# Down projection: operand pairs of the first group made inside the direct column jobs; final rows: a group's squares issued after the next group's roundings

## The chip, the core and the metric

The kernel runs on one core of a Trainium2 chip. A core has five engines with their own in-order instruction streams: TensorE (PE in the profile, with its weight loads as PEld), VectorE (DVE), ScalarE (ACT), GpSimd (POOL) and SyncE (SP). Here SP only issues transfers, and POOL issues those that add into their destination. The metric is the device time of one execution in microseconds; the time before is the median of three runs.

## The reference, cut to what matters

One encoder layer on 512 tokens of width 2048, all in float32. The first part (normalisation, input projection, two kinds of sequence mixing, output projection, residual) is not touched. The change lies in the last part:

```python
h = rmsnorm(x, ffn_norm_w[l])
x = x + (jax.nn.silu(h @ w_gate[l]) * (h @ w_up[l])) @ w_down[l]
return rmsnorm(x, final_norm_w)
```

`w_gate` and `w_up` are 2048 x 5632, `w_down` is 5632 x 2048. With g for the product in the brackets, the down projection is g (512 x 5632) times `w_down`. The result is added to x, and every row is then normalised over its 2048 values.

## The kernel before, in words

**Precision.** A float32 operand is rounded to a high part on ACT (a copy to the fp32r type), and DVE subtracts that from the operand to give the low part. A product is then three matmuls: high by high, high by low, low by high. So each operand that reaches PE has first cost one ACT instruction and one DVE instruction. The text calls this pair of instructions a rounding.

**How w_down is tiled.** The 5632 rows of `w_down` are 44 tiles of 128 rows, taken as 22 pairs of tiles, numbered 0 to 21. The 2048 output columns are four column blocks c of 512. g lies in device memory, one pair to an entry (`gd`).

- *Pairs 0 and 1: the direct column jobs.* Four jobs, one for each c (`run_job`, L273; its matmuls are L303 to L305). A job has four steps i, one for each tile, and each step is 12 matmuls over 512 columns. Ahead of step i come `before_down` (L1463) and then `st.split`, which rounds the half piece of `w_down` that is used two or three steps later (L201 on ACT, L202 on DVE). At the job's end `evac_down` (L1457) copies four PSUM banks out with ACT, and POOL adds them into `xd`.
- *Pairs 2 to 19: the class `Down`.* It uses a seven-product scheme in place of eight on 2 x 2 blocks. For each pair q, seven operands are formed from g (B11, B21, B22, T1 to T4), and for each pair and column block the weights get sums of their own. One step i of `run` (pair q, column block c) is 7 x 2 x 3 = 42 matmuls over 256 columns (L1625 to L1627). The steps follow in ten runs r: X = pairs 2 to 7 for c = 0, 1, 2; X and Y = pairs 8 to 14 for c = 3; Y for c = 2 and 1; Y and Z = pairs 15 to 19 for c = 0; Z for c = 1, 2 and 3. The operands of X thus serve runs 0 to 3.
- *Pairs 20 and 21: the final rows* (`finish`), described below.

**What a step of Down needs.** The weights of step i are loaded (L1141, SP), summed (`sums`: L1157 to L1159, DVE) and rounded (`split`: L1169 on ACT, L1174 on DVE) up to three steps ahead, in the shared slots `s4` (20 of 128 x 1024). Four of these slots hold the weights of a step until its matmuls have read them, and the roundings for a later step go into slots set free in that way. The operands of a pair come out of the generator `operands` (from L1534), one piece of work for each call of `make`:

- the first call only loads two pairs of g (L1542, SP);
- step 1 of a pair: four 128 x 256 additions or subtractions on DVE (L1556 to L1559);
- step 2: two roundings (L1568 and L1569, and a first L1571 and L1572), and the load of a further pair;
- step 3: two more roundings (L1571, L1572). The next call enters the pair in `self.x` and goes on to step 1 of the next pair.

Before a pair is begun, the generator asks that its number is not above `self.upto` and that at least `self.gap` (13) of the 62 slots `s2` (128 x 512) are free. Otherwise the call does nothing. A pair keeps seven `s2` slots until its last run. `make(1)` is called once in the last unit of the gate and up products (`down_start`, L1434) and once in each of the 16 steps of the direct jobs (`before_down`). `run` calls it, behind the roundings of the weights, until the pair of its step is there, and then up to two times more.

`self.upto` is 0 when `Down` is built, and the first pair has the number 2. `run` sets it before each step: to 14, the last pair of Y, up to run 5, and to 19 from run 6 on.

**The final rows.** `finish` takes the 512 tokens as four rows t of 128. A group is one row and one column block: 12 matmuls over 512 columns (`products`, L1797 to L1799), then `residual` (L1449, DVE, reads the bank and adds into x1), then `squares` (L409, ACT, the sum of squares of the result). Rows 0 and 1 go together through the four column blocks, then row 2, then row 3. The last eight half pieces of `w_down` are rounded (L201, L202) in the first four groups, two to a group. `later` (L1780 to L1785) ends a row: the reciprocal root from the four sums of squares (ACT and DVE, one element to a partition), four multiplications on DVE (L1784) and the stores on SP. `run_urgent` puts left-over work of the last run of `Down` between the groups (L1689, DVE).

Engines take their instructions in the order in which the program issues them, and slots are handed out and put back in that order too; an instruction that writes a slot waits until the last readers of it are done.

Of the kernel before, what the change touches and what calls it, by code (L numbers as in the profile page):

```python
# [114 lines left out]
def put(*slots):  # L115
    for s in slots:
        if s.home is not None:
            s.home.free.append(s.i)


def layer(nc, tc, x, attn_norm_w, w_in, rel_table, gw_f, gb_f, gw_b, gb_b, gla_norm_w, w_out,
# [7 lines left out]
    with tc.manual_schedule(), \  # L129
# [30 lines left out]
        class Stream:  # L160


            def __init__(self):
                self.pieces = []
                self.halves = []
                self.n_dma = self.n_conv = 0
                self.limit = 3
                self.held = 0
                self.until = None
                self.big = None  # L170
# [38 lines left out]
        st = Stream()  # L209
# [25 lines left out]
        def run_urgent():  # L235
            while urgent:
                try:
                    next(urgent[0])
                    break
                except StopIteration:  # L240
                    urgent.popleft()
# [165 lines left out]
        def squares(c, t, tiles, ss):  # L407
            junk = s2.get()
            act.activation(junk.t, tiles[t].t, AF.Square, accum_out=ss[:, t * 4 + c:t * 4 + c + 1])  # L409
            put(junk)  # L410
# [3 lines left out]
        ss2, sum2, rstd2 = small[:, 32:48], small[:, 48:52], small[:, 52:56]  # L414
# [593 lines left out]
        x1 = {}  # L1008
# [472 lines left out]
        class Down(Blocks):  # L1481
# [3 lines left out]
            def __init__(self, X, Y, Z):  # L1485
                self.runs = [(0, X), (1, X), (2, X), (3, X + Y), (2, Y), (1, Y), (0, Y + Z), (1, Z), (2, Z), (3, Z)]
                self.pairs = X + Y + Z
                self.drop = {q: r for r, part in ((3, X), (6, Y), (9, Z)) for q in part}
                self.begin([(r, q) for r, (c, part) in enumerate(self.runs) for q in part], 1, 256)
                self.x, self.parts, self.m, self.pre, self.seen = {}, {}, {}, [], set()  # L1490
                self.most, self.upto, self.gap = 4, 0, 13
                self.making = self.operands()

            def source(self, r, q):
# [200 lines left out]
            def run(self):  # L1695
                for i, (r, q) in enumerate(self.seq):
                    c, part = self.runs[r]
                    n = part.index(q)
                    left = len(part) - 1 - n if self.summed(r) else None
                    self.load()  # L1700
                    self.sums(i)
                    self.split(i)
                    if left != 0:
                        self.sums(i + 1)
                        if r > 6 and n == 0:
                            self.split(i + 1)
                        self.sums(i + 2)
                        self.split(i + 1)
                        self.part(i + 3)
                        if left == 1:  # L1710
                            self.split(i + 2)
                            self.sums(i + 3)
                        elif r != 3 and not self.by_dma(i + 2) and len(s4.free) > 4:
                            self.sums(i + 3)
                            self.split(i + 2)
                    self.upto = self.pairs[-1] if r > 5 else self.runs[4][1][-1]
                    while q not in self.x:
                        self.make(1)
                    self.gap = 10 if r == 6 else 13
                    self.make(2 if r == 3 else (r == 6) + i % 2)  # L1720
                    if n == max(len(part) - 5, 0) and r + 1 < len(self.runs) and self.summed(r + 1):
                        self.fetch(r + 1)
                    if self.summed(r) and n == (1 if r == len(self.runs) - 1 else len(part) - 2):
                        x1[c] = [s2.get() for _ in range(4)]
                        for t in range(4):
                            pool.dma_start(out=x1[c][t].t, in_=xd[4 * c + t])
                    self.products(i)
                    if left == 0:
                        self.part(i + 3)
                    else:  # L1730
                        run_urgent()
                    if r == len(self.runs) - 1:
                        if n == 0:
                            g_load(LAST // 2)
                            g_load(LAST // 2 + 1)
                        if n == 1:
                            st.until, st.limit, st.big = None, 1, tail_first
                            st.load()
                            g_split(LAST // 2)
                        if n == 2:  # L1740
                            g_split(LAST // 2 + 1)
                            st.limit = 4
                            st.split(tail_first + 2)
                        if n == 3:
                            st.split(tail_first + 8)
# [24 lines left out]
        def finish():  # L1770
# [5 lines left out]
            upto = [first + 8]  # L1776
# [11 lines left out]
            def products(t, c, b, cols):  # L1788
                tok = slice(t * P, (t + 1) * P)
                o = b.t[:, cols]  # L1790
                for k in range(per):
                    if t < 2 and k % 2:
                        upto[0] += 1
                        st.split(upto[0])
                    _, _, wh, wl = st.halves[first + c * per + k]
                    xh, xl = gT[LAST + k]
                    mm(o, xh.t[:, tok], wh.t[:, cols], start=k == 0, stop=False, skip_group_check=True)  # L1797
                    mm(o, xh.t[:, tok], wl.t[:, cols], start=False, stop=False, skip_group_check=True)
                    mm(o, xl.t[:, tok], wh.t[:, cols], start=False, stop=k == per - 1, skip_group_check=True)  # L1799
# [8 lines left out]

            def run():
                whole = slice(0, 512)  # L1810
                for rows in ((0, 1), (2,)):
                    for c in range(4):
                        for t in rows:
                            b = ps.get()
                            products(t, c, b, whole)
                            run_urgent()
                            residual(c, t, b)
                            squares(c, t, x1[c], ss2)
                    for t in rows:
                        ys = [s2.get() for _ in range(4)]  # L1820
                        later(t, ys)
                        put(*ys, *(x1[c][t] for c in range(4)))
                t = 3
                ys = []
                sm, m, r, q = sum2[:, t:t + 1], scr[0][:, 0:1], rstdf[:, t:t + 1], scr[1][:, 0:1]
                for c in range(4):
                    ys.append(s2.get())
                    for n in range(2 if c == 3 else 1):
                        cols = slice(256 * n, 256 * n + 256) if c == 3 else whole
                        b = ps.get()  # L1830
                        products(t, c, b, cols)
                        if c == 3 and n == 1:
                            dve.tensor_reduce(sm, ss2[:, 11:15], op=OP.add, axis=mybir.AxisListType.X)
                            dve.tensor_scalar(sm, sm, 1.0 / D, EPS, op0=OP.mult, op1=OP.add)
                        at_ = 11 + c + n
                        part(t, c, b, cols, ss2[:, at_:at_ + 1], ys[c])
                dve.tensor_scalar(m, ss2[:, 15:16], 1.0 / D, sm, op0=OP.mult, op1=OP.add)
                act.activation(q, m, AF.Ln)
                act.activation(r, q, AF.Exp, scale=-0.5)
                dve.scalar_tensor_tensor(q, r, m, r, op0=OP.mult, op1=OP.mult)  # L1840
                dve.tensor_scalar(q, q, -0.5, 1.5, op0=OP.mult, op1=OP.add)
                dve.tensor_tensor(m, r, q, op=OP.mult)
                for c in (1, 0, 2, 3):
                    o = ys[c]
                    if c == 1:
                        act.activation(o.t, o.t, AF.Copy, scale=m)
                    else:
                        dve.tensor_scalar(o.t, o.t, m, None, op0=OP.mult)
                    (act if c in (1, 3) else sp).dma_start(
                        out=out[t * P:(t + 1) * P, c * 512:(c + 1) * 512], in_=o.t)  # L1850
                put(*ys, *(x1[c][t] for c in range(4)))
# [48 lines left out]
```

## Time and profile before

| | |
|---|---|
| time, median of 3 runs | 2218.49 us (2217.82 to 2223.97) |
| profiled execution: its time | 2222.8 us |
| profiled execution: span of the trace | 2221.0 us |
| mean granted TensorE clock | 0.993 of full speed |
| busy: PE | 2184.1 us (98%) |
| busy: PEld | 1921.2 us (87%) |
| busy: DVE | 1587.3 us (71%) |
| busy: ACT | 1228.8 us (55%) |
| busy: POOL | 329.1 us (15%) |

All times are microseconds from the start of the span. The view by stretches gives the busy time of each engine within a stretch, with the number of instructions in brackets, then the granted TensorE clock (PEclk), the busy share of the DMA engines and the rate moved. The view by time has a row for an instruction, or for several of a kind, with its start, its length and, in square brackets, the idle time of its engine before it and what ended this. The view by groups gives the number of instructions of a line, their busy time, the mean length of one in ns, and the idle time before them. Instructions that follow each other overlap a little on PE, DVE and ACT, so the distance between two starts is shorter than the length that is given.

In this execution the direct column jobs run from 1723.6 to 1766.97, `Down` from there to 2165.28, and the final rows from 2165.28 to the end.

### The profile page before, as it was taken

The page shows a single profiled execution, that of the slowest core. Times are in us where ns is not written, and L with a number is a line of the kernel's source. Part 1 is how long each engine was busy: PE and PEld are TensorE (multiplying, and loading weights), DVE is VectorE, ACT ScalarE, POOL GpSimd, SP SyncE. Part 2 cuts the span into 40 slices and gives each one's busy share as a digit, 9 for nine tenths or more (in the row PEclk, how much of TensorE's full clock was granted, in tenths as well). Part 3 has the DMA queues.
Part 4 walks back from the last instruction along what each step waited for, and adds up shares of the span by engine and source line. Part 5 has one row for each costly group of instructions (what it writes and reads, how often), then busy time and mean ns, then how long its engine had stood idle before and what let it go on. Part 6 is the DMA issues. An engine that isn't in the chain of part 4 may idle for free.

```text
span 2221.0 us, 33659 instructions
## 1 busy us (share of the span) xinstructions
PE 2184.1 (98%) x12594; PEld 1921.2 (87%) x12594; DVE 1587.3 (71%) x2757; ACT 1228.8 (55%) x2040; POOL 329.1 (15%) x363
## 2 busy tenths in 40 slices
PE   9999999999999999999999999999999879999998
PEld 7888888888888888888888888888888679999996
DVE  4366665755566447888888888888888576878987
ACT  5344454444556346666666666666665544745653
POOL 0000000000000111222222222222222201211110
PEclk9999999999999999999999999999999979999999
DMA  6525634323234425898898888889888835958882
GB/s 207 159 84 148 166 91 132 93 86 95 86 95 158 155 83 138 192 209 202 198 207 197 203 204 206 200 200 208 200 205 221 189 133 153 271 163 220 239 288 102
DMA packets 256467, 376.78 MB, mean 170 GB/s; under 512 B 18063, under 2 KB 179519, under 8 KB 256304
## 3 DMA queue, kind: packets, MB, share of 16 engines
q1 hardware_dynamic: 188768, 252.03, 36.2%
q0 software_dynamic: 66352, 121.55, 28.1%
q8 instruction: 99, 1.62, 0.3%
q10 hardware_dynamic: 1184, 1.06, 0.1%
q14 instruction: 64, 0.52, 0.1%
HBM read 246.58 MB, written 35.19 MB: 127 GB/s over the span
## 4 chain that ended last, share of the span: by engine, by line
PE 91%; DVE 3%; issue 2%; DMA 1%; ACT 1%; POOL 1%; SPq 0%; DVEq 0%; ACTq 0%; POOLq 0%
PE pd L1302 22%; PE pd L1308 11%; PE ps L303 5%; PE ps L304 5%; PE ps L305 5%; PE ps L295 5%; PE ps L296 5%; PE ps L297 5%; PE pu L1627 5%; PE pu L1626 5%; PE pu L1625 5%; PE pe L1302 4%; PE pe L1308 2%; PE ps L529 1%; PE ps L537 1%
## 5 line engine op out<-in xcount | busy, mean ns | idle before, releaser
L1302 PE MATMUL pd<-a,b 128*128 128x512 f32 x2112 | 528.4, 392 | 0.8 <-DVE a L1063 0.8
L1302 PEld LDWEIGHTS pd<-a,b 128*128 128x128 f32 x2112 | 378.9, 188 | 67.0 <-DVE a L1063 1.2
L1308 PEld LDWEIGHTS pd<-a,b 128*128 128x128 f32 x2112 | 288.5, 190 | 21.6
L1625 PE MATMUL pu<-b,a 128*128 128x256 f32 x1008 | 290.2, 288 | 14.2 <-ACT a L1568 11.1
L1627 PE MATMUL pu<-b,a 128*128 128x256 f32 x1008 | 290.2, 288 | 7.9 <-DVE a L1569 6.0
L1308 PE MATMUL pd<-a,b 128*128 128x256 f32 x2112 | 294.9, 282 | 0.0
L202 DVE TENSOR_TENSOR a<-b,a 128x512 fp32r<-128x512 f32 x273 | 183.3, 686 | 151.6 <-ACT a L201 139.3
L1626 PE MATMUL pu<-b,a 128*128 128x256 f32 x1008 | 289.6, 287 | 0.4 <-DVE b L1174 0.4
L1209 POOL DMA_DIRECT2D b<-b x176 | 209.8, 1248 | 520.8 <-ACT b L1208 390.8
L1247 ACT CAST b<-b 128x1024 fp32r<-128x1024 f32 x176 | 185.3, 1053 | 166.2 <-DVE b L1233 138.5
L1248 DVE TENSOR_TENSOR b<-b,b 128x1024 fp32r<-128x1024 f32 x176 | 214.9, 1221 | 50.2 <-ACT b L1247 26.4
L1625 PEld LDWEIGHTS pu<-b,a 128*128 128x128 f32 x1008 | 197.9, 196 | 15.6 <-ACT a L1568 12.2
L1627 PEld LDWEIGHTS pu<-b,a 128*128 128x128 f32 x1008 | 197.9, 196 | 9.5 <-DVE a L1569 7.0
L1626 PEld LDWEIGHTS pu<-b,a 128*128 128x128 f32 x1008 | 197.9, 196 | 0.6 <-DVE b L1174 0.6
L201 ACT CAST a<-b 128x512 fp32r<-128x512 f32 x273 | 161.5, 618 | 46.4 <-PE ps L305 22.3
L1330 DVE TENSOR_TENSOR a<-pd,a 128x512 f32<-128x512 f32 x132 | 91.4, 692 | 95.7 <-ACT a L1329 95.7
L1208 ACT ACTIVATE b<-b 128x768 fp32r<-128x768 f32 x176 | 149.3, 848 | 4.7 <-PE ps L305 2.9
L1210 ACT CAST b<-b 128x768 fp32r<-128x768 f32 x176 | 145.4, 826 | 0.6 <-PE ps L305 0.6
L1329 ACT COPY a<-pd 128x512 f32<-128x512 f32 x132 | 77.6, 588 | 101.9 <-PE pd L1308 101.9
L1169 ACT CAST b<-b 128x768 fp32r<-128x768 f32 x88 | 78.8, 940 | 99.6 <-issue 77.3
L1174 DVE TENSOR_TENSOR b<-b,b 128x768 fp32r<-128x768 f32 x88 | 94.3, 1090 | 46.2 <-ACT b L1169 42.5
L1230 DVE TENSOR_TENSOR b<-b 128x512 f32<-128x512 f32 x176 | 120.4, 684 | 0.0
(284 smaller groups left out, 4419.0 us busy)
## 6 DMA issues: line engine op xcount, KB each, us to landing
b<-b POOLq DMA_DIRECT2D x204, 384.0 KB, 5.8
b<-in_w_gate_dram SPq DMA_DIRECT2D x88, 512.0 KB, 4.2
b<-in_w_up_dram SPq DMA_DIRECT2D x88, 512.0 KB, 4.5
b<-in_w_down_dram SPq DMA_DIRECT2D x88, 512.0 KB, 5.8
b<-in_w_in_dram SPq DMA_DIRECT2D x48, 512.0 KB, 4.6
b<-in_w_in_dram SPq DMA_DIRECT2D x94, 256.0 KB, 4.2
b<-in_w_out_dram SPq DMA_DIRECT2D x32, 512.0 KB, 5.6
a<-a SPq DMA_DIRECT2D x96, 128.0 KB, 2.4
```

The costliest lines, as they stand in the source:

```text
L201: act.copy(h[2].t, r)
L202: dve.tensor_tensor(h[3].t, r, h[2].f, op=OP.subtract)
L1208: act.activation(lo.t, r, AF.Copy, scale=-1.0)
L1209: pool.dma_start(out=lo.f, in_=r, accum_op=OP.add)
L1210: act.copy(hi.t, r)
L1247: act.copy(hi.t, self.S[i].t)
L1248: dve.tensor_tensor(lo.t, self.S[i].t, hi.f, op=OP.subtract)
L1302: mm(o, wh.t[:, p, k], x_.t.rearrange("p s t -> p (s t)"), start=first and p == 0, stop=False, skip_group_check=True)
L1308: mm(o[:, 256:512], wl.t[:, p, k], x_.t[:, 0], start=False, stop=last and p == 1, skip_group_check=True)
L1625: mm(o, xh[:, t], wh, start=first and not loaded and h == 0, stop=False, skip_group_check=True)
L1626: mm(o, xh[:, t], wl, start=False, stop=False, skip_group_check=True)
L1627: mm(o, xl[:, t], wh, start=False, stop=last, skip_group_check=True)
```

## The change: what it does

`Down` is built with `self.upto` at 14, the last pair of Y. `run` sets `self.upto` from run 6 on alone. So a call of `make` in the direct jobs no longer does nothing, where 13 slots are free.

In the final rows, both roundings of a group are issued ahead of its 12 matmuls, where they stood ahead of the second and the fourth tile; they are the same instructions, and on ACT and DVE they keep their order among themselves. The squares of a group are put on a list and issued after the residual of the next group, that is, behind the roundings of the next group. The last squares of a set of rows are issued before `later`.

```diff
@@ class Down, __init__
-                self.most, self.upto, self.gap = 4, 0, 13
+                self.most, self.upto, self.gap = 4, Y[-1], 13
@@ class Down, run
-                    self.upto = self.pairs[-1] if r > 5 else self.runs[4][1][-1]
+                    if r > 5:
+                        self.upto = self.pairs[-1]
                     while q not in self.x:
                         self.make(1)
@@ finish, products
+                if t < 2:
+                    upto[0] += 2
+                    st.split(upto[0])
                 for k in range(per):
-                    if t < 2 and k % 2:
-                        upto[0] += 1
-                        st.split(upto[0])
                     _, _, wh, wl = st.halves[first + c * per + k]
@@ finish, run
                 whole = slice(0, 512)
+                todo = deque()
                 for rows in ((0, 1), (2,)):
                     for c in range(4):
                         for t in rows:
                             b = ps.get()
                             products(t, c, b, whole)
                             run_urgent()
                             residual(c, t, b)
-                            squares(c, t, x1[c], ss2)
+                            if todo:
+                                squares(*todo.popleft())
+                            todo.append((c, t, x1[c], ss2))
+                    squares(*todo.popleft())
                     for t in rows:
```

## The prediction

> **What bounds the kernel now.** I read the page first, then the busy time by stretches, then the groups within the one stretch where PE is not full, and last the rows by time around its gaps.
>
> ```profile
> span 2221.0 us, 33659 instructions
> ```
>
> ```profile
> core 0: us, PE busy (x) PEld busy (x) DVE busy (x) ACT busy (x) POOL busy (x), PEclk, DMA share, GB/s
> 1723.60:1734.48 10.88, 10.88 (x50) 9.00 (x49) 8.11 (x14) 5.48 (x10) 1.59 (x3) 1.00 0.92 356
> 1734.48:1745.36 10.88, 10.88 (x50) 9.01 (x49) 2.50 (x4) 4.80 (x9) 3.54 (x5) 1.00 0.68 98
> 1745.36:1756.24 10.88, 10.88 (x50) 9.01 (x49) 2.50 (x4) 4.80 (x9) 3.52 (x5) 1.00 0.66 96
> 1756.24:1766.97 10.73, 10.73 (x49) 8.68 (x47) 7.74 (x13) 5.40 (x9) 3.37 (x5) 1.00 0.82 147
> 1766.97:1832.00 65.03, 42.96 (x254) 40.18 (x254) 49.37 (x89) 28.77 (x48) 5.21 (x9) 0.79 0.49 142
> 1832.00:1862.15 30.15, 30.15 (x254) 30.15 (x253) 23.43 (x32) 15.21 (x22) 3.45 (x8) 1.00 0.43 135
> 2165.28:2189.60 24.32, 22.79 (x99) 17.79 (x98) 19.29 (x30) 12.86 (x28) 0.00 (x0) 1.00 0.17 63
> 2189.60:2211.66 22.06, 22.06 (x109) 18.58 (x107) 18.58 (x42) 6.71 (x22) 0.00 (x0) 1.00 0.40 143
> ```
>
> The first four rows are the four direct column jobs. PE is busy throughout, while in the second and third DVE works 2.50 us of 10.88. The fifth row is run 0 of `Down`: six steps, 252 matmuls, in 65.03 us at a mean clock of 0.79. The sixth row is the next six steps: the same 254 records in 30.15 us at full clock (0.1196 us a matmul, 5.02 us a step). So run 0 takes 65.03 - 30.15 = 34.9 us more than the same work does right behind it. The seventh row is the first eight groups of the final rows: 24.32 us, with PE idle for 1.5.
>
> Groups within 1766.97 to 1832:
>
> ```profile
> L1625 PE MATMUL pu<-b,a 128*128 128x256 f32 x85 | 29.0, 342 | 14.2 <-ACT a L1568 11.1 <-ACT a L1571 3.0
> L1627 PE MATMUL pu<-b,a 128*128 128x256 f32 x84 | 28.7, 342 | 7.9 <-DVE a L1569 6.0 <-DVE a L1572 1.8
> ...
> L1174 DVE TENSOR_TENSOR b<-b,b 128x768 fp32r<-128x768 f32 (+1 forms) x14 | 15.1, 1091 | 14.8 <-ACT b L1169 14.8
> ...
> L1572 DVE TENSOR_TENSOR a<-a,a 128x512 fp32r<-128x512 f32 x12 | 7.7, 686 | 0.0
> L1571 ACT CAST a<-a 128x512 fp32r<-128x512 f32 x12 | 6.9, 614 | 3.3 <-DVE a L1557 3.1 <-DVE a L1559 0.2
> ...
> L1556 DVE TENSOR_TENSOR a<-b 128x256 f32<-128x256 f32 x7 | 2.9, 420 | 0.0
> L1558 DVE TENSOR_TENSOR a<-b,a 128x256 f32<-128x256 f32 x7 | 2.9, 420 | 0.0
> L1569 DVE SCALAR_TENSOR_TENSOR a<-b,a 128x256 fp32r<-128x256 f32 x7 | 2.9, 419 | 0.0
> L1557 DVE TENSOR_TENSOR a<-b 128x256 f32<-128x256 f32 x7 | 2.9, 419 | 0.0
> L1568 ACT ACTIVATE a<-b 128x256 fp32r<-128x256 f32 x7 | 2.9, 412 | 0.0
> ```
>
> All of PE's idle time, 14.2 + 7.9 = 22.1 us, ends with a rounding of a pair's operands (L1568, L1569, L1571, L1572), none with weights. The other 34.9 - 22.1 = 12.8 us are matmuls at a lowered clock after these gaps.
>
> Why a pair is late at each step shows on ACT:
>
> ```profile
> 1784.07 1.78 ACT L1169 CAST b<-b 128x768 fp32r<-128x768 f32 x2 [7.52 <-PE pu L1627]
> 1785.75 0.41 ACT L1568 ACTIVATE a<-b 128x256 fp32r<-128x256 f32 x1
> 1786.07 0.60 ACT L1571 CAST a<-b 128x512 fp32r<-128x512 f32 x1
> ```
>
> ```profile
> 1786.22 0.39 PE L1625 MATMUL pu<-b,a 128*128 128x256 f32 x1 [2.23 <-ACT a L1568]
> ```
>
> L1169 rounds the weights of a step three ahead into slots that the finished step sets free, so ACT stands still until PE is through. The roundings of the pair that PE wants next are queued behind it. PE and ACT take turns, step after step.
>
> **The pairs, part by part.** The first call of `make` only loads. The 16 calls in the direct jobs then do three steps to a pair: pairs 2 to 6 are finished by the sixteenth call, which also does step 1 of pair 7. Slots: following the handing out and putting back in the code, the direct jobs leave 45 of the 62 `s2` slots free at the first call, 49 through the middle, and 51, 53 and 57 at the last three. With seven held for each finished pair, pair 6 begins with 49 - 28 = 21 free and pair 7 with 57 - 35 = 22; 13 are asked for, so every call does its step. Pair 7 gets its second and third steps in steps 1 and 3 of run 0 and is used in step 5. At the end of step 5 both kernels stand at the same place (pair 8 after its second step, 10 slots free); from there on the program is the same.
>
> *Cost of what moves.* By the rows above, a pair takes on DVE 4 x 0.42 + 0.42 + 3 x 0.69 = 4.2 us, on ACT 0.41 + 3 x 0.61 = 2.2 us. A job holds 4/3 of a pair: 5.5 us of DVE and 3.0 of ACT. Jobs 1 and 2 then have DVE 2.50 + 5.5 = 8.0 and ACT 4.80 + 3.0 = 7.8 of 10.88 us: room to spare. Job 0 and job 3 are tight, 8.1 + 5.5 and 7.7 + 5.5 = 13.6 and 13.2, over their own length by 2.7 and 2.3; job 0's overhang runs into the room of job 1. Half pieces are rounded two to three tiles (5.4 to 8.2 us) before PE needs them. Laying the moved steps in the order of issue into the gaps of DVE, the tightest ones in job 0 come out 0.5 to 0.9 us ahead of PE. I cost the direct jobs at 0, with bounds 0 and 3 us (the overhang of job 0, fully exposed); no gain is possible there, since PE is full.
>
> *Start of run 0.* Nothing of a pair stands any longer between the jobs and step 0; its weights are rounded within job 3, by my layout at 1766.1, with PE through with the jobs at 1766.97. Step 1 starts at 1772.0.
>
> ```profile
> 1767.76 3.44 ACT L1169 CAST b<-b 128x768 fp32r<-128x768 f32 x4
> 1771.10 0.41 ACT L1568 ACTIVATE a<-b 128x256 fp32r<-128x256 f32 x1
> ```
>
> The L1169 of its weights follows the evacuation of job 3, as before. The first two L1174 then take DVE to about 1770.8, or 1771.2 with the overhang: 0.8 us ahead. The next step has 2 us more. Bounds: 0 and 2.3 us (job 3's overhang); I take 0.
>
> *Steps 2 to 5.* In run 0, DVE was busy for 49.37 us, of which seven pairs are 7 x 4.2 = 29.4. The remaining 20 us and what is left of pairs (steps 2 and 3 of pair 7, 1 and 2 of pair 8: about 5 us) fit into 30.15. L1169 will still wait for the end of a step, but for a use two steps (10 us) later, with at most 1.8 us of ACT and 2.2 of DVE to do. The sixth row above runs in just that order without a gap. So the six steps take 30.15 us, and this part gives 34.9; bounds 34.9 - 3 - 2.3 = 29.6 and 34.9 (all the excess is gone then).
>
> *SP and the DMAs.* Five loads of pairs (4 to 8, 512 KB each) move into the direct jobs and ahead of loads of `w_down` in SP's order. Their slots are taken from 13 to 17 free ones, the longest free first, not from the pair in work. A 512 KB load took 9.0 us in this stretch (row below); the pieces behind them are wanted a job (10.88 us) or more later, and the DMA engines are at 0.66 to 0.82 in jobs 1 to 3. POOL gets nothing new. Cost 0; the upper bound is the third rival's.
>
> ```profile
> b<-in_w_down_dram SPq DMA_DIRECT2D x13, 512.0 KB, 9.0
> ```
>
> **The final rows.** Placing both roundings ahead of the matmuls changes nothing: they are on ACT and DVE, the matmuls on PE, and no order on any engine changes. The squares do:
>
> ```profile
> 2175.75 0.63 ACT L409 ACTIVATE a<-a 128x512 f32<-128x512 f32 x1 [5.39 <-DVE a L1449]
> 2176.28 0.19 ACT L409 ACTIVATION_READ_ACCUMULATOR a<-a 128x1 f32 x1
> 2176.38 1.13 ACT L201 CAST b<-b 128x512 fp32r<-128x512 f32 x2
> ```
>
> ```profile
> 2177.01 1.29 DVE L202 TENSOR_TENSOR b<-b,b 128x512 fp32r<-128x512 f32 x2 [1.30 <-ACT b L201]
> ```
>
> ```profile
> 2184.87 0.50 PE L1797 MATMUL pu<-b,a 128*128 128x512 f32 x1 [1.11 <-ACT b L201]
> 2185.60 0.50 PE L1798 MATMUL pu<-b,a 128*128 128x512 f32 x1 [0.23 <-DVE b L202]
> ```
>
> ```profile
> 2189.79 0.75 DVE L1449 SCALAR_TENSOR_TENSOR a<-pu,small,a 128x512 f32<-128x512 f32 x1 [1.01 <-PE pu L1799]
> ```
>
> The next group's L201 waits behind the squares, these wait for DVE's residual, and DVE's L202 then idles 1.30 us for L201. This happens three times, 3.9 us on DVE, until PE itself stalls. Behind the change L201 is done before the residual, and the last L202 comes about 3.9 us earlier, at about 2182.1. PE wants it at 2183.7: it no longer stops. Eight groups of 12 matmuls need 8 x 2.72 = 21.8 us (four direct tiles of 12 make 10.88, one 2.72) and took 24.32: 2.5 us. The last residual of rows 0 and 1 waits for PE, so DVE's chain behind it, which sets the end, moves by the same. What is late next is PE alone. Bounds 0 (the slots for L201 come free no earlier) and 2.5; I take 2.5.
>
> **Sum.** 34.9 + 2.5 = 37.4 us off the profiled execution: span 2221.0 - 37.4 = 2183.6. That execution's own time, 2222.8, goes to 2185.4; it is 4.3 above the median of the runs, 2218.49, to which I apply the difference: **2181 us**.
>
> **Rivals.**
>
> *A short stall remains.* Job 3's overhang (2.3 us) makes PE wait at step 0 or 1, and the clock drops once. For: the margins of 0.5 to 0.9 us come from a layout by hand, not from a row. Against: each tile has rounded halves two tiles ahead. What a gap does to the clock shows in step 5 of run 0:
>
> ```profile
> 1823.48 0.58 PE L1625 MATMUL pu<-b,a 128*128 128x256 f32 x1 [2.23 <-ACT a L1568]
> ```
>
> ```profile
> 1823.48:1832.00 8.52, 8.03 (x43) 7.74 (x44) 6.95 (x14) 5.75 (x11) 2.54 (x5) 0.61 0.82 280
> ```
>
> After 2.23 us of waiting, this step ran at a mean clock of 0.61 and took 8.52 us where 5.02 are its length at full clock; with 0.5 us more of idle time in it, the clock cost 3.0. The rival's time is 2181 + 2.3 + 3.0 = 2186. The Trainium skill, "TensorE: Matmul & The Clock Gate", section "What's actually happening", says that the clock is halved after at least one idle window, given as about 3.4 us. The trace has a drop behind a shorter gap than that, so here the row decides; by the page a gap of 2.3 us would keep the clock, and the rival would stand at 2183.
>
> *The steps of run 0 become paced by DVE and the weights.* If DVE has to wait for ACT in run 0 as it did before (14.8 us before L1174, above), its 25 us of work become 40, and PE follows: 10 us of the gain are lost, 2191. For: the slots of a step's weights are still the ones that PE sets free. Against: the sixth row of the stretches, with the same order and no gap.
>
> *The final rows give nothing*, because L201 waits for its slots: 2183.6. For it speaks that the last slots were read by the matmuls just before; against it that these end at 2165.28, ten microseconds ahead of the rounding at 2176.38.
>
> *The change doesn't do what it says*: the calls in the jobs find too few free slots and return at once, and only the 2.5 us come off: 2216. My count leaves 21 and 22 against 13.
>
> *SP stands still: slower.* The place is SP's order in the direct jobs. Each of the five moved loads waits for a slot that the pair in work still holds, and the pieces of `w_down` behind it with it. PE then waits out a load, 9.0 us, and pays the clock, 3.0: 5 x 12 = 60 us against 37.4 of gain, 2241. It decides from 37.4 / 5 = 7.5 us a load. For: such waits exist,
>
> ```profile
> SPq L1542 <- DVE a L1569: 2.2, 2, 1.1
> ```
>
> (1.1 us at the longest, over 1700 to 1850), in run 0, where one slot or two are free. Against: in the direct jobs 13 or more are.
>
> **How the numbers follow.** Forecast 0.72 (2178 to 2184.5); short stall 0.11; paced by DVE 0.07; final rows without gain 0.03; no effect 0.03; SP 0.04. The range of 2177.5 to 2190 holds the first, second and fourth, 0.86, and after the scatter of the runs shown (2217.8 to 2224.0) about 8 in 10; its lower end is the sum with all bounds at their best and 3.5 us for the scatter, its upper end the sum with the direct jobs and the start at their worst (5.3 us) and a clock drop (3.0). A measurement of this kernel can tell about 0.3%, 6.7 us, from no change. Faster by more: 0.72 + 0.11 + 0.07 + 0.03 = 0.93; within it: 0.03; slower: 0.04.
>
> **What would show each step right or wrong.** In the profile of the changed kernel: L1556 to L1572 of five pairs during the direct jobs, with PE full in all four and DVE near 8 us in jobs 1 and 2; 252 matmuls of run 0 in 30 to 31 us behind the last L305, at full clock, with no wait for L1568 to L1572; L1169 still waiting for L1627, and PE not for L1174. In the final rows: L201 of the second group right behind that of the first, no 1.30 us before L202, eight groups in 21.8 us, and the stretch from there to the end as long as before. The prediction is wrong if PE has gaps within the direct jobs (then the moved work was too much for DVE there), if run 0 is over 36 us, or if a stretch that has no part in the change grows.

## The result, and the profile after

The changed kernel takes 2185.92 us (median of 5 runs, 2185.1 to 2188.29) against 2219.41 (median of 5, 2217.82 to 2224.86): a ratio of 0.9845 with a 95% interval of 0.9828 to 0.9861, that is 34 us less (31 to 38). The span of the profiled execution went from 2221.0 to 2183.3 us. The prediction was 2181, with 2177.5 to 2190 as its range.

The first line of the page, after:

```profile
span 2183.3 us, 33662 instructions
```

Busy time by stretches, after: the four direct jobs together, run 0 of `Down`, the six steps behind it, and the final rows from their first matmul to the start of the last residual of rows 0 and 1.

```profile
core 0: us, PE busy (x) PEld busy (x) DVE busy (x) ACT busy (x) POOL busy (x), PEclk, DMA share, GB/s
1722.61:1766.13 43.52, 43.52 (x194) 36.03 (x193) 38.04 (x75) 29.88 (x55) 11.99 (x15) 1.00 0.86 226
1766.13:1796.37 30.24, 30.24 (x254) 30.23 (x252) 29.20 (x47) 18.10 (x27) 4.13 (x7) 1.00 0.69 185
1796.37:1826.61 30.24, 30.24 (x255) 30.24 (x253) 25.45 (x37) 15.82 (x23) 4.62 (x10) 1.00 0.54 182
2130.07:2152.06 21.99, 21.99 (x99) 18.21 (x98) 18.62 (x30) 12.58 (x27) 0.00 (x0) 1.00 0.16 62
```

Run 0 takes 30.24 us at full clock where it took 65.03, just as long as the six steps behind it. The direct jobs are not longer (43.52; before, from the first L303 at 1723.44 to 1766.97, 43.53), although they now hold 38.04 us of DVE, where the four rows of before add up to 20.85. The stretch of the final rows is 21.99 us long; before it was 2189.79 - 2165.28 = 24.51.

PE's waits from 1700 to 2200, after, all of them:

```profile
PE pu L1626 <- DVE b L1174: 0.4, 1, 0.4
PE pu L1626 <- DVE b L1528: 0.2, 1, 0.2
```

Where 22.1 us of waiting for a pair's roundings stood in run 0 alone, 0.6 us is left from 1700 to the end. On ACT (rows by time, after) L1169 still comes at the end of each step, but now nothing that PE wants soon is queued behind it:

```profile
1771.41 1.79 ACT L1169 CAST b<-b 128x768 fp32r<-128x768 f32 x2 [0.99 <-ACT b L1169]
1773.11 0.41 ACT L1568 ACTIVATE a<-b 128x256 fp32r<-128x256 f32 x1
1773.42 0.60 ACT L1571 CAST a<-b 128x512 fp32r<-128x512 f32 x1
1776.45 1.78 ACT L1169 CAST b<-b 128x768 fp32r<-128x768 f32 x2 [2.43 <-issue]
1781.49 1.79 ACT L1169 CAST b<-b 128x768 fp32r<-128x768 f32 x2 [3.26 <-issue]
1783.19 1.13 ACT L1571 CAST a<-a 128x512 fp32r<-128x512 f32 x2
1786.53 1.79 ACT L1169 CAST b<-b 128x768 fp32r<-128x768 f32 x2 [2.22 <-issue]
```

L1169 comes every 5.04 us, the length of a step, and always 0.24 us behind the first matmul of the next step (1771.17, 1776.21, 1781.25 and 1786.29). That it waits for PE is read from this: the rows themselves give "issue" as what ended the idle time, as most of those of before do; only the wait of 7.52 us there names PE. The L1568 and L1571 between are those of pair 7, which PE wants at step 5 only (1791.33).

The final rows on ACT, after: the roundings of the first two groups follow each other, and the squares come behind them.

```profile
2133.52 2.18 ACT L201 CAST b<-b 128x512 fp32r<-128x512 f32 x4
2140.05 0.63 ACT L409 ACTIVATE a<-a 128x512 f32<-128x512 f32 x1 [4.35 <-DVE a L1449]
```

On DVE, after, L202 of the second group stands right behind the residual, with no idle time before it (1.30 us before), and the last residual of rows 0 and 1 still waits for PE:

```profile
2139.93 1.28 DVE L202 TENSOR_TENSOR b<-b,b 128x512 fp32r<-128x512 f32 x2
...
2152.06 0.75 DVE L1449 SCALAR_TENSOR_TENSOR a<-pu,small,a 128x512 f32<-128x512 f32 x1 [1.97 <-PE pu L1800]
```

From this residual to the end it is 2183.3 - 2152.06 = 31.24 us; before, 2221.0 - 2189.79 = 31.21.

### The profile page after: what moved, and what is told of

Its sections match the earlier page's. It is cut to its first block, busy times and chain, and to the rows that moved or that the text cites. A ratio compares the mean times of both kernels' runs of the same rounds, so it can differ in the third digit from the quotient of the medians.

```text
span 2183.3 us, 33662 instructions
## 1 busy us (share of the span) xinstructions
PE 2170.7 (99%) x12594; PEld 1911.7 (88%) x12594; DVE 1585.7 (73%) x2757; ACT 1227.9 (56%) x2040; POOL 328.9 (15%) x363
## 4 chain that ended last, share of the span: by engine, by line
PE 96%; DVE 2%; DMA 1%; ACT 1%; issue 0%; ACTq 0%; DVEq 0%; SPq 0%
PE pd L1302 22%; PE pd L1308 12%; PE ps L303 5%; PE ps L304 5%; PE ps L305 5%; PE ps L295 5%; PE pu L1626 5%; PE ps L297 5%; PE ps L296 5%; PE pu L1627 5%; PE pu L1625 5%; PE pe L1302 4%; PE pe L1308 2%; PE ps L529 1%; PE ps L537 1%; PE ps L538 1%
## 5 line engine op out<-in xcount | busy, mean ns | idle before, releaser
L1626 PE MATMUL pu<-b,a 128*128 128x256 f32 x1008 | 285.5, 283 | 0.6 <-DVE b L1174 0.4
L1627 PE MATMUL pu<-b,a 128*128 128x256 f32 x1008 | 285.3, 283 | 0.0
L1625 PE MATMUL pu<-b,a 128*128 128x256 f32 x1008 | 285.2, 283 | 0.0
L202 DVE TENSOR_TENSOR a<-b,a 128x512 fp32r<-128x512 f32 x273 | 183.7, 686 | 131.8 <-ACT a L201 120.9
L1626 PEld LDWEIGHTS pu<-b,a 128*128 128x128 f32 x1008 | 193.5, 192 | 1.0 <-DVE b L1174 0.6
L1625 PEld LDWEIGHTS pu<-b,a 128*128 128x128 f32 x1008 | 193.5, 192 | 0.0
L1627 PEld LDWEIGHTS pu<-b,a 128*128 128x128 f32 x1008 | 193.5, 192 | 0.0
L1169 ACT CAST b<-b 128x768 fp32r<-128x768 f32 x88 | 78.9, 942 | 79.9 <-issue 68.1
L595 ACT CAST b<-ps 128x512 fp32r<-128x512 f32 x64 | 37.6, 587 | 142.9 <-PE ps L529 142.9
```

Source lines behind the costliest of these rows:

```text
L202: dve.tensor_tensor(h[3].t, r, h[2].f, op=OP.subtract)
L1625: mm(o, xh[:, t], wh, start=first and not loaded and h == 0, stop=False, skip_group_check=True)
L1626: mm(o, xh[:, t], wl, start=False, stop=False, skip_group_check=True)
L1627: mm(o, xl[:, t], wh, start=False, stop=last, skip_group_check=True)
```

## The experiments

All times are set beside runs of the kernel before on the same chip as the experiment: its median was 2222.94 us (17 runs, 2217.68 to 2225.28) for the first four, 2222.57 (8 runs, 2218.15 to 2224.94) for the other four. The lengths of run 0 are taken from the end of the direct jobs to the first matmul of run 1.

### The pairs alone, and the squares alone

Each half of the change by itself: the edits in `Down` without those in `finish`, and the reverse.

> Only the pairs are made in the direct column jobs; the final rows stand as before. Theory (ACT's queue: a pair's roundings stood behind weight roundings that wait for PE): run 0 of Down takes 30.15 us at full clock and the kernel is 31 to 35 us faster than before, about 2.5 us above the whole change (2188.4 against 2185.9). Rival (the end is set elsewhere and the squares carry nothing): the same time as the whole change, 2185.9. In the trace the stretch from the first matmul of the final rows to the last residual of rows 0 and 1 is 24.5 us by the theory, 22.0 by the rival.

> Only the final rows are changed; the pairs are made as before. Theory: 2.5 us faster than before, 2216.9, with 22.0 us from the first matmul of the final rows to the last residual of rows 0 and 1 and no matmul there waiting for L201 or L202. Rival (nothing, as DVE sets the end anyway): 2219.4. It also is a second execution of run 0 of Down as before: 65.0 us again if that length is fixed; between 60 and 65 if the part of it that is lost to the clock differs from execution to execution, which would explain that the medians differ by 33.5 and the two profiled executions by 37.7.

The pairs alone: 2187.54 us, ratio 0.9844 (0.9832 to 0.9857), 35 us less than before. The squares alone: 2220.02 us, ratio 0.9988 (0.9978 to 0.9998), 2.7 us less (0.4 to 4.9). The stretch from the first matmul of the final rows to the last residual of rows 0 and 1, with the pairs alone, then with the squares alone:

```profile
2130.91:2155.07 24.16, 22.85 (x99) 18.06 (x98) 18.91 (x30) 12.50 (x27) 0.00 (x0) 1.00 0.16 60
```

```profile
2167.79:2189.77 21.98, 21.98 (x99) 18.22 (x98) 18.59 (x30) 12.58 (x27) 0.00 (x0) 1.00 0.17 66
```

In the traces the two parts are independent of each other: the stretch is 24.2 to 24.5 us without the moved squares and 22.0 with them, whatever was done to the pairs, and the rival that the squares carry nothing falls. The times say less. The ratio of the pairs alone, 0.9844, is that of the whole change, 0.9845, so beside the moved pairs the 2.5 us of the squares can't be told from the scatter; alone they come out at 2.7 us, with an interval that nearly reaches nothing. The other edit in `finish` (roundings ahead of the matmuls) was not run by itself. By the program, ACT, DVE and PE each keep their instructions and their order with it.

Run 0 with the squares alone is run 0 as it was before, in another execution:

```profile
1767.55:1834.37 66.82, 44.57 (x254) 42.01 (x253) 49.36 (x89) 28.76 (x48) 5.20 (x9) 0.74 0.47 134
```

It took 66.8 us at a mean clock of 0.74, against 65.03 at 0.79. The length of this stretch isn't fixed. This matters for the sum below.

### One pair, three pairs

As the whole change, but only pair 2, or pairs 2 to 4, may be made in the direct jobs:

```diff
-                self.most, self.upto, self.gap = 4, Y[-1], 13
+                self.most, self.upto, self.gap = 4, X[0], 13    # and X[2]
...
-                    if r > 5:
-                        self.upto = self.pairs[-1]
+                    self.upto = self.pairs[-1] if r > 5 else self.runs[4][1][-1]
```

> As the whole change, but only pair 2 may be made in the direct jobs; pairs 3 to 7 come in run 0 as before. By the steps of the trace of before, the excess over 5.02 us is 12.0, 5.3, 1.5, 7.3, 3.0 and 5.7 us for steps 0 to 5. Theory (each step pays by itself, and the first pays most): 12.0 of 34.9 are gone, run 0 takes 53 us, and the time is the whole change plus 22.9, 2209. Rival (the gain goes by the number of pairs moved, a sixth each): the whole change plus 29, 2215. Second rival (the loss is the cold start, and once PE is going the steps run through): near 2186.

> As the whole change, but only pairs 2, 3 and 4 may be made in the direct jobs. Theory (each step pays by itself): steps 0 to 2 run at 5.02 us, steps 3 to 5 keep their excess of 16.0 us, so the time is the whole change plus 16, 2202, and run 0 takes 46 us. Rival (by number): the whole change plus 17.4. Second rival (the loss is the cold start): near 2186.

One pair: 2214.55 us, ratio 0.9967 (0.9954 to 0.998), run 0 in 60.5 us. Three pairs: 2200.42, ratio 0.9905 (0.9891 to 0.992), run 0 in 44.75. The times forecast stand on the 2185.9 us of the whole change, which was run apart from these (the kernel before had 2219.4 there and has 2222.9 here), so the gains over before are compared, each with the 2.5 us of the squares. With one pair the kernel is 7 us faster than before (4 to 10). The rival by number has 5.8 + 2.5 = 8.3 and is right; my theory has 12.0 + 2.5 = 14.5 and is wrong, as is its 53 us for run 0. The idea that only a cold start is lost (37) is wrong in both. Three pairs, 21 us faster (18 to 24), don't tell the first two apart (21.4 and 20). (The excess by step in the expectation is cut at PE's waits: the stretch given as step 1 holds 54 matmuls and that of step 2 31, where a step has 42. The sums used, 12.0 and 16.0, aren't touched by this.) Why the first pair saves so little shows on ACT and on PE, with one pair made ahead:

```profile
1774.53 0.41 ACT L1568 ACTIVATE a<-b 128x256 fp32r<-128x256 f32 x1
1774.85 0.60 ACT L1571 CAST a<-b 128x512 fp32r<-128x512 f32 x1
1779.39 0.62 ACT L1571 CAST a<-a 128x512 fp32r<-128x512 f32 x1 [3.94 <-DVE a L1557]
```

```profile
1780.54 0.58 PE L1627 MATMUL pu<-b,a 128*128 128x256 f32 x1 [5.04 <-DVE a L1569]
```

Step 0 runs through, and the wait that was its own (4.44 and 4.21 us before) comes back at step 1, as 2.23 and 5.04: pair 3 is begun behind the roundings of the weights of three steps, which stand close together at the start, on DVE as on ACT. The long wait goes with the first pair that is made within run 0, not with step 0. It is shorter the later that pair comes: with three pairs made ahead it is 2.23 and 2.13 us, at step 3.

### The same work in another order

The kernel before, with nothing moved into the direct jobs; in run 0 the pair of the step and the next one are made ahead of the sums and roundings of the weights.

```diff
                     left = len(part) - 1 - n if self.summed(r) else None
+                    if r == 0:
+                        self.upto = self.runs[4][1][-1]
+                        for p_ in part[n:n + 2]:
+                            while p_ not in self.x:
+                                self.make(1)
                     self.load()
```

> The kernel before, with one change of order: in run 0 the operands of a step's pair and of the next pair are made ahead of the weights' sums and roundings of that step, so that they no longer stand behind L1169 on ACT. No work moves into the direct jobs, and the final rows are as before. Theory (the order on ACT makes PE and ACT take turns): run 0 is then bound by DVE, whose work there is 49.4 us, and takes 48 to 53 us in place of 65; the time is 2203 to 2208. Rival (the amount of work is what counts, the order doesn't): run 0 stays at 60 to 65 us and the time at 2217 to 2221.

2200.65 us, ratio 0.9906 (0.9891 to 0.9921), 21 us less than before. Run 0:

```profile
1767.54:1808.94 41.40, 34.75 (x253) 32.41 (x253) 39.51 (x75) 24.60 (x40) 2.67 (x4) 0.96 0.55 159
```

The rival (the amount of work counts, not its order) falls: the pairs are still made in run 0 (only the four additions of pair 2 begin 1.5 us ahead of it), and 65 us become 41.4. DVE is then busy for 39.51 of these and is the bound, as expected. Run 0 came out shorter than the 48 to 53 us expected because part of the 49.4 us of DVE that I counted is for the steps behind run 0 and doesn't hold up its own: 11 of L1174 and 5 of L1157 now fall into run 0, where 14 and 7 did. So most of the loss of run 0, 24 of 35 us, was the place of the pairs' roundings in the queues; 1.3 us of it come back in the first step of run 1, which takes 6.35 us where 5.02 is its length. The other 11 us are still lost in this order; moving the work out of run 0 takes them away too.

### The clock kept up

The kernel before, with matmuls added in the waits of run 0. Their results are used by nothing.

```diff
+                fill(36 if i == 0 else 18)
                 for n, ((wh, wl), x) in enumerate(prods):
...
                         mm(o, xh[:, t], wl, start=False, stop=False, skip_group_check=True)
+                        if n == 0 and h == 0:
+                            fill(34 if i == 0 else 5)
                         mm(o, xl[:, t], wh, start=False, stop=last, skip_group_check=True)
```

Here `fill(k)` issues k matmuls over 256 columns into a spare bank in run 0 and nothing elsewhere.

> The kernel before, with matmuls added in run 0 whose results are used by nothing: 70 in step 0 (36 ahead of its first matmul, 34 ahead of the first that waits for the low part) and 23 in each other step (18 and 5), at 0.12 us each about as long as the waits in the trace. The order of all else stays. Theory (22.1 us of run 0 are waiting and 12.8 us are the lowered clock behind the waits): the clock stays at full speed, run 0 takes about 52 us and the time is 2206. Rival (the lowered clock was hidden behind the same chain of ACT and DVE, which sets the pace): run 0 stays above 60 us, and the time is 2217 or more, since the added matmuls only take up waiting time.

2213.29 us, ratio 0.9962 (0.9948 to 0.9976), 8 us less than before (5 to 12), with 185 matmuls more. Run 0:

```profile
1767.02:1824.41 57.39, 55.87 (x439) 53.12 (x438) 48.90 (x88) 28.67 (x48) 5.19 (x9) 1.00 0.52 151
```

The result lies between the two theories. The clock stays at 1.00, and run 0 goes from 65 or 67 us to 57.4, not to 52. So 7.6 to 9.4 us, by which of the two executions it is set against, were lost to the lowered clock, and not 12.8.

That is what the rows by time of before give too, when the slow matmuls are counted instead of taken as a remainder:

```profile
1778.16 0.41 PE L1626 MATMUL pu<-b,a 128*128 128x256 f32 x1
1778.37 0.41 PE L1627 MATMUL pu<-b,a 128*128 128x256 f32 x1
...
1788.92 0.28 PE L1626 MATMUL pu<-b,a 128*128 128x256 f32 x1
1789.30 0.39 PE L1627 MATMUL pu<-b,a 128*128 128x256 f32 x1
```

While the clock is at 0.50 (first two rows), matmuls of run 0 start 0.213 us apart, where 0.120 us is the distance at 1.00. There are 88 of them before, 8.2 us in all, and 105 with the squares alone, 9.8 us. The other 4 to 5 us of the 12.8 are short pauses where matmuls stop and start again, as in the last two rows: 0.38 us from start to start at clock 1.00, with no wait named. The added matmuls don't take these away: run 0 is 57.4 - 30.2 = 27 us over its own matmuls, 22.1 of it the added ones (185 at 0.12), 0.6 named waits, and some 4 to 5 us pauses (in this trace one from 1777.76 to 1778.15, for example).

The spread also changes: five runs lie between 2212.76 and 2213.96 us, 1.2 us apart, where the eight runs of before beside them spread over 6.8 us. The 17 runs of before beside the first experiments fit this: the three shortest (2217.68, 2218.21 and 2218.57 us) have a mean clock of 0.995 over the whole span, the longest (2225.28) has 0.991.

### More work for DVE in the direct jobs

The whole change, with one or two additions of 128 x 512 behind each call of `make` in the direct jobs. Their results are used by nothing.

```diff
                 dn.make(1)
+                for _ in range(1):    # and range(2)
+                    d = s2.get()
+                    dve.tensor_tensor(d.t, gT[3][0].f, gT[3][0].f, op=OP.add)
+                    put(d)
```

> The whole change, with one addition of 128 x 512 on DVE (0.6 us, its result is used by nothing) behind each of the 16 calls of make in the direct jobs: 9.6 us more of DVE. The trace of the whole change has DVE busy for 38.0 us of the direct jobs' 43.4 and 29.1 of run 0's 30.15, together 67.1 of 73.5. Theory (DVE is the cover that is left, 6 us of it): 76.7 against 73.5, so PE waits 1 to 5 us and the time is 2186 to 2191. Rival (the roundings two tiles ahead take it up): 2186 and no waits of PE.

> The whole change, with two such additions behind each call: 19.2 us more of DVE, whose results are used by nothing. Theory (DVE's cover is about 6 us): 67.1 + 19.2 = 86.3 against 73.5, so PE loses 10 to 16 us, with a drop of the clock where a single wait reaches 2 us: 2196 to 2204. Rival (another cover): 2186 to 2189.

One: 2187.33 us, ratio to before 0.9847 (0.9832 to 0.9862). Two: 2197.21, ratio 0.9892 (0.9877 to 0.9907), by the ratios 10 us above the whole change. PE's waits from the direct jobs through run 0, with one addition, then with two:

```profile
PE pu L304 <- DVE a L202: 1.1, 2, 0.8
PE pu L1630 <- DVE b L1174: 0.3, 1, 0.3
```

```profile
PE pu L304 <- DVE a L202: 5.5, 7, 1.4
PE pu L1630 <- DVE b L1174: 2.8, 2, 1.9
```

The direct jobs and run 0, with two additions:

```profile
1722.93:1775.00 52.07, 46.61 (x192) 34.82 (x192) 51.79 (x98) 30.38 (x54) 12.07 (x15) 1.00 0.71 182
1775.00:1808.54 33.54, 30.74 (x254) 30.26 (x253) 32.79 (x51) 18.26 (x27) 4.05 (x6) 1.00 0.63 158
```

The theory holds: DVE is what the moved work uses up, and with two additions it is busy for 51.79 of 52.07 us and sets the pace. 19.2 us more of DVE cost 52.07 + 33.54 - 43.52 - 30.24 = 11.9 us, so the cover that the change leaves in these two stretches is about 7 us (6 expected). (The first row starts 0.16 us behind the first matmul of the jobs.) One addition, 9.6 us, makes PE wait 1.4 us in the trace, and the same two stretches are 45.71 and 30.75 us long, 2.7 more than with the change alone: again about 7 us of cover. Its time differs from that of the whole change by less than its interval.

## Why the prediction was right, and where its size was off

**What bounds run 0: right.** The pairs' roundings stood behind L1169, which waits for PE. The trace after has no such wait, and the experiment with the other order shows it as the cause, since it removes most of the loss while the pairs stay in run 0.

**The split of the 34.9 us: mis-read, without effect on the sum.** "The other 34.9 - 22.1 = 12.8 us are matmuls at a lowered clock after these gaps": counted by rows, the slow matmuls are 8.2 us, and 4 to 5 us are pauses where matmuls stop and start. The whole excess goes with the waits, so the sum doesn't use the split; the expectation of the clock experiment does, and was off by it.

**34.9 us for the pairs: right in the trace.** From the first matmul of the direct jobs to the first of the final rows it was 2165.28 - 1723.44 = 441.8 us and is 2130.07 - 1722.61 = 407.5: 34.4 less. Of the 0.5 that is missing, 0.4 lies in the steps behind run 0 (333.70 us to the final rows, 333.28 before), where the two waits of 0.4 and 0.2 us are.

**The direct jobs at 0: right.** PE has no wait there. DVE is busy for 9.38 and 8.71 us in jobs 1 and 2 (8.0 predicted), ACT for 7.44 and 7.81 (7.8):

```profile
1733.49:1744.37 10.88, 10.88 (x49) 9.01 (x48) 9.38 (x20) 7.44 (x15) 4.95 (x7) 1.00 1.01 280
1744.37:1755.25 10.88, 10.88 (x49) 9.01 (x48) 8.71 (x18) 7.81 (x15) 3.58 (x6) 1.00 0.68 100
```

The overhang didn't come: jobs 0 and 3 hold 10.70 and 9.25 us of DVE, where 13.6 and 13.2 were added up. The margin is thin all the same: with one instruction more on DVE for each call, PE waits at job 1 already (0.33 and 0.75 us).

**DVE in run 0: mis-sized.** "The remaining 20 us and what is left of pairs (...: about 5 us) fit into 30.15": DVE was busy for 29.20 us there, not 25. I had taken durations (seven pairs at 4.2 us) from a busy time, and in these views instructions that follow each other overlap (a 128x512 subtraction on DVE is shown with 0.69 us, and the next one starts 0.60 us after it): the busy time counts an overlap once, the durations count it twice. Part of what was added up too much in the direct jobs is the same. By the groups after, the weights alone are 14.7 + 4.8 + 3.0 + 3.0 = 25.5 us in run 0 and the pairs 5.9, together 31.4 for those 29.20:

```profile
L1174 DVE TENSOR_TENSOR b<-b,b 128x768 fp32r<-128x768 f32 (+1 forms) x14 | 14.7, 1086 | 0.3 <-ACT b L1169 0.3
L1157 DVE TENSOR_TENSOR b<-b 128x512 f32<-128x512 f32 x7 | 4.8, 689 | 0.2
L1158 DVE TENSOR_TENSOR b<-b,b 128x256 f32<-128x256 f32 x7 | 3.0, 425 | 0.2
L1159 DVE TENSOR_TENSOR b<-b,b 128x256 f32<-128x256 f32 x7 | 3.0, 425 | 0.2
```

It still fitted, with 1 us to spare where I had seen 5.

**2.5 us for the squares: right.** 24.51 to 21.99 us in the same stretch, and the end moved by as much.

**The sum: 37.4 us predicted for the profiled execution, 37.7 measured** (34.4 + 2.5, and 0.8 that the part ahead of the direct jobs, which the change doesn't touch, took less in this execution).

**The step that failed: "it is 4.3 above the median of the runs, 2218.49, to which I apply the difference".** It gave 2181, and 2185.9 was measured. The profiled execution was a long one (2222.8), and what lengthens an execution of the kernel before is, as far as the runs show, the clock within run 0: 65.0 and 66.8 us in two profiled executions, and a spread of 1.2 us in place of 6.8 once the clock is kept up there. The change takes this stretch away with its scatter. So the 4.3 us were, by this account, contained in the 37.4 and were subtracted twice; the difference taken from the profiled execution's own time, 2222.8 - 37.4 = 2185.4, is 0.5 us from the median measured. That run 0 is where the 4.3 us lie in that very execution is inferred from these numbers; no trace of a short execution of the kernel before was taken. The median of three was also a low one: with two runs more it is 2219.41.

**The rivals.** The short stall at the start didn't come (0.3 us before L1174 on DVE and nothing on PE). Its price of 3.0 us for the clock is one outcome of several: waits of 2.23 and 0.78 us left the clock at 1.00 in step 1 of before (last section). Pacing by DVE didn't come, but was nearer than thought (29.20 of 30.24). The calls did their steps, and SP didn't hold anything up: its loads of pairs waited 5.6 us in all from 1700 to 1800, and PE waited for no transfer.

## What to carry to other kernels

An instruction that waits for the slowest engine's progress stops everything that is queued behind it on its own engine; what PE wants next belongs ahead of it, in order or in time, and the order alone was worth 24 of the 35 us of run 0 here. Before work is moved into a stretch where PE is full, count the free time there of the engines that do it: here DVE had enough with 7 us to spare, and two instructions more for each call cost the kernel 10 us. When the stretch that a change removes is also the one that scatters, apply the difference to the profiled execution's own time and not to the median. And count what a lowered clock costs from the matmuls themselves: what is left after the waits holds other things too.

## What the runs showed of the hardware

At a granted clock of 0.50 the matmuls over 256 columns start 0.213 us apart, at 1.00 they start 0.120 us apart.

Waits well below the 4.44 and 4.21 us at the start of run 0 can lower the clock too, but they don't do it each time. Step 1 of run 0 has the same two waits, 2.23 and 0.78 us, in the traces of two kernels that are alike up to there. Before, then with the squares alone:

```profile
1783.99:1792.76 8.77, 5.66 (x42) 5.25 (x43) 7.72 (x14) 4.47 (x8) 0.00 (x0) 1.00 0.53 180
```

```profile
1783.29:1793.20 9.91, 6.91 (x42) 6.71 (x43) 8.23 (x15) 4.47 (x8) 0.00 (x0) 0.83 0.47 160
```

In the first the clock stays at 1.00, in the second the step has a mean of 0.83 and is 1.1 us longer. Step 5 of before, with 2.23 and 0.48 us of waiting, has 0.61. So the length of a wait alone doesn't tell here what it will cost; what does was not tested. How much is lost differs from execution to execution (0.74 or 0.79 over the whole of run 0). The times of the kernel before, 7 to 8 us apart, go with the mean clock of the span (0.995 in the shortest runs, 0.991 in the longest).

Keeping PE busy with matmuls whose results nothing uses took this away: the kernel was 8 us faster and its runs lay within 1.2 us, although 22 us of matmuls were added.
